# Dilated heads with the values as weights, and a mixture of dilations made on turned tiles

## The chip, the core and the metric

One Trainium2 chip, of which one core is used. The metric is the device time of one execution in microseconds. The engines are TensorE (PE, with PEld for the loading of its weights), VectorE (DVE), ScalarE (ACT), GpSimd (POOL) and SyncE (SP); POOL and SP issue DMAs here.

## What is computed

One layer of an encoder and its final norm, in float32, over 1280 tokens of 1024 features: a sample of 1024 tokens and a prompt of 256. The part that matters is the dilated branch and what follows it:

```
def _dilated_mixture(q, k, v, bias_b):
    outs, lses = [], []
    for gi, (window, dil) in enumerate(((128, 1), (512, 4), (2048, 16))):
        hs = slice(gi * 4, (gi + 1) * 4)
        o, lse = _banded_attention(residues(q[:, :, hs], dil), residues(k[:, :, hs], dil),
                                   residues(v[:, :, hs], dil), window // (2 * dil), dil, bias_b[:, hs], None)
        outs.append(from_residues(o, dil)); lses.append(from_residues(lse, dil))
    alpha = softmax(stack(lses), axis=0)
    return sum(alpha[..., None] * stack(outs), axis=0)

h = rmsnorm(x, g_mix); z = h @ w_in           # queries, keys, values of both branches, two gates
merged = gate_a * (o_a @ w_branch_a) + gate_b * (o_b @ w_branch_b)
x = x + merged @ w_out
x = x + square(relu(rmsnorm(x, g_mlp) @ w_up)) @ w_down
```

There are three groups (dilations 1, 4 and 16) of four heads of 64 features. `lse` is the maximum plus the logarithm of the sum of exponentials. The mixture weighs, for each token and each of the four heads, the three groups' outputs by the softmax of the three `lse`. The other branch, o_a, is an attention over a window of 128 with 8 heads.

## The kernel before

Large products are split into a high and a low part in the reduced format fp32r, three matmuls each (hi by lo, lo by hi, hi by hi), and those of w_in, w_up and w_down are combined in seven products for eight blocks. The work is written in the order in which it stands on each engine; generators that hand over with `yield` put one stage's steps between another's. The stages, by the profile's time: the norm and the values until about 120 us; pairs of columns of w_in until 355 us; the same pairs with the dilated heads between them until 535 us; the last pair until 560 us; windowed attention with the logits of the remaining gate columns as PE's filling until about 712 us; gates and branches until about 860 us; then w_out, w_up and w_down.

**The dilated heads** (`attention_b`, L482) have 60 tiles of 128 queries: an outer loop over the two pairs of heads i, then the groups 2, 1, 0, then the tiles of a group. Two tiles make a step, and a step is put at every second `tick` of the pairs' products. A step loads values for the present tiles (L503), multiplies the probabilities of the two tiles of two steps before with their values (`values_of`, L558), copies the results out and stores them (`store_values`, L570), turns the probabilities of the tiles before (L553, tile pt), and makes the scores (L522) and exponentials (L543) of the present ones. A tile's window is 128 or 256 keys wide; in group 2 a sample's tile consists of two pieces of 64 queries. In `values_of` the turned probabilities are PE's weights and the 64 columns of a head's values are streamed, so the result has queries in the partitions. Two tiles share a bank of PSUM (pv). A tile's results, its negated maxima (nm) and its sums (l) lie beside each other in a row of 132 numbers (o) and go to DRAM with one or two DMAs of POOL (L575) into `scr_b` of the group.

**Windowed attention** (from L1047) runs in a loop over j = 0, 2, ... 40 with two of 40 tiles each, four units of queries and ten tiles in a unit. In each iteration, in this order on PE: a part of the logits of the gates (`logits`, L1124, matmuls at L192), the values of an earlier tile (`values_of`, L1099; here the values are the weights, L1110, and the two heads of a pair have the upper and the lower half of the output's partitions), the turns (L1095), the scores (L1071), then the same for the second tile. Weights for the logits are split by ACT (whi, L231) and DVE (wlo, L235); ACT also makes the gates' column sums ready (gs, L1135), and the copies of turned probabilities are divided between ACT (L271) and DVE (L273).

**The mixture** runs beside that loop, a step at each half of an iteration from j = 4 on (`next(merges)`). For two tiles and one pair of heads, `load_rows` (L1140) fetches the rows of the three groups with eight DMAs of POOL for a sample's pair of tiles and six for the prompt's, each of them undoing the dilation; `merge` (L1162) makes the three weights of each row (L1167 to L1178, with the exponential on ACT), multiplies (L1182) and adds (L1187, L1188) on DVE. At the end of the loop and in the gate stage, PE turns the merged tiles (`turn_merged`, L1209, tile tm, 20 transposes), ACT makes the high part out of PSUM (L1224) and DVE the low part (L1228); both undo, in their order of columns, what the order of rows has left of the dilation. The gate stage puts these calls between its products by a table, `side`, from product number to calls.

POOL also issues the stores of windowed attention's results (`scr_o`, L1114) and the loads of its biases (L454 to L468), and makes the differences of w_in's blocks (L393). PSUM is handed out in banks by tag; "mm" is the tag of the large products.

Of the kernel before, what the change touches and what calls it, by code (L numbers as in the profile page):

```python
# [15 lines left out]
P = 128  # L16
# [3 lines left out]
T = NS + NP  # L20
# [9 lines left out]
ROW = 2 * HD + 4  # L30
# [67 lines left out]
def encoder_kernel(  # L98
# [97 lines left out]
    def run(gen):  # L196
        for _ in gen:
            pass
# [56 lines left out]
    l_a = const.tile([P, AH, NT], F32, name="l_a")  # L255

# [20 lines left out]
    scr_b = [dram.tile([T, 2, ROW], F32, name=f"scr_b{g}_") for g in range(3)]  # L277
# [204 lines left out]
    def attention_b(make):  # L482
# [5 lines left out]
        held, live, bias = {}, {}, {}  # L488
        turned_s = slot("pt", (P, 2, 4, P))
# [22 lines left out]
        def scores(j):  # L512
# [12 lines left out]
            for k in (j, j + 1):  # L525
# [5 lines left out]
                o = make("o", (P, ROW), n=8)  # L531
# [3 lines left out]
                nc.vector.tensor_scalar(o[:, 2 * HD : 2 * HD + 2], m, -1.0, None, op0=ALU.mult)  # L535
                live[k] = s, o

        def exponentials(j):
            W = order[j][3][1]
            s, o = live[j]  # L540
            nm, l = o[:, 2 * HD : 2 * HD + 2], o[:, 2 * HD + 2 :]
# [4 lines left out]
        def transposes(j, eng):  # L546
            W = order[j][3][1]
            s, o = live[j]
# [7 lines left out]
            live[j] = pt, o  # L556

        def values_of(j, whole):  # L558

            _, _, _, (pieces, W, _) = order[j]  # L560
            pt, v = live[j][0], held.pop(j)[1]
            pv = whole[:, P * (j % 2) : P * (j % 2) + P]
            for h in range(2):
                for a, (p0, nq, _, _) in enumerate(pieces):
                    for k in range(W // P):
                        nc.tensor.matmul(pv[p0 : p0 + nq, HD * h : HD * h + HD], pt[:, 2 * k + h, p0 : p0 + nq],  # L566
                                         v[:, a + k, HALVES[h]], start=k == 0, stop=k == W // P - 1,
                                         skip_group_check=True)

        def store_values(j, eng, whole):  # L570
            g, i, _, (pieces, _, _) = order[j]
            o = live.pop(j)[1]
            moved(eng, o[:, : 2 * HD], whole[:, P * (j % 2) : P * (j % 2) + P])
            for p0, nq, qa, _ in pieces:
                nc.gpsimd.dma_start(scr_b[g][qa : qa + nq, i, :], o[p0 : p0 + nq, :])  # L575
# [8 lines left out]
        for j in range(0, n + 4, 2):  # L584
            load_v(j)
            load_v(j + 1)
            if j > 2:
# [3 lines left out]
                store_values(j - 4, nc.scalar, pv)  # L591
                store_values(j - 3, nc.vector, pv)
# [456 lines left out]
    if True:  # L1049
# [90 lines left out]
        def load_rows(i, t):  # L1140

            r = rows_b[i, t] = wslot("r", (P, 2, 3, ROW))
            for j in range(2):
                if t < 8:
# [740 lines left out]
```

## Time and profile before

| | us |
|---|---|
| median of 3 runs | 1723.69 (1723.07 to 1723.81) |
| profiled execution | 1723.0 |
| its span, first to last instruction | 1721.2 |
| PE busy | 1690.8 |
| DVE, ACT, POOL busy | 973.6, 727.0, 516.2 |
| PE idle in the stage of windowed attention, 560 to 700 us | 2.23 of 140 |
| DVE, ACT, POOL busy in the same 140 us | 90.9, 81.7, 55.3 |

The granted clock of TensorE was 0.999 over the span. The profiled execution's time is 1.8 us more than its span, and 0.7 us below the median of the runs. In the profile, a line such as "L566 PE MATMUL pv<-v,pt x384" names a source line, an engine, an operation, the tile written and the tiles read; for PE the later tile of the two may be either the weights or what is streamed. [...] In the chain that ended last, each piece has a start, a length and a count; in the waits there stand a total, a count and the longest one.

### The profile page before, as it was taken

The numbers are of one execution on the slowest core, as the hardware profiler recorded it, in microseconds if no ns is written. First come the engines' busy times: TensorE is split into PE (matmuls) and PEld (weight loads), VectorE is DVE, ScalarE is ACT, GpSimd is POOL, SyncE is SP. The second block draws the span as 40 slices with busy tenths as digits, with TensorE's granted clock in tenths as the row PEclk, the third lists the DMA queues.
The fourth block names the chain that finished last, engine by engine and source line by source line (L and its number), as shares of the span: only waits on it lengthen the run. The fifth ranks groups of instructions, "written<-read, shape, count | busy, mean of one in ns | idle before, by whom it ended". The sixth has DMA issues, their size and how long they took to land.

```text
span 1721.2 us, 25157 instructions
## 1 busy us (share of the span) xinstructions
PE 1690.8 (98%) x9248; PEld 1430.4 (83%) x9248; DVE 973.6 (57%) x1688; ACT 727.0 (42%) x1528; POOL 516.2 (30%) x442
## 2 busy tenths in 40 slices
PE   7999999999999999999999999999999999999998
PEld 6898888888888888788888788888888888888886
DVE  6732323445553566677368545455556876667575
ACT  6232323355553555655166333333334433333344
POOL 0213222212322244300100445565555342314140
PEclk9999999999999999999999999999999999999999
DMA  6414343576666753656012334433446834633333
GB/s 239 145 43 140 115 137 95 150 196 178 173 171 176 208 174 104 221 181 230 25 74 74 122 120 157 149 115 127 157 136 232 308 130 158 209 115 117 117 116 123
DMA packets 213738, 256.34 MB, mean 149 GB/s; under 512 B 24487, under 2 KB 144123, under 8 KB 213488
## 3 DMA queue, kind: packets, MB, share of 16 engines
q1 hardware_dynamic: 200704, 228.26, 41.1%
q0 software_dynamic: 11824, 24.38, 4.6%
q10 hardware_dynamic: 1088, 2.10, 0.3%
q8 instruction: 73, 1.20, 0.3%
q14 instruction: 49, 0.40, 0.1%
HBM read 169.10 MB, written 90.73 MB: 151 GB/s over the span
## 4 chain that ended last, share of the span: by engine, by line
PE 87%; DVE 4%; ACT 2%; issue 2%; DMA 2%; POOL 1%; SPq 0%; DVEq 0%; ACTq 0%; POOLq 0%
PE dn L351 21%; PE x L351 18%; PE mm L192 12%; PE z L351 9%; PE v L739 5%; PE pv L351 5%; PE mm L351 5%; PE y L351 4%; PE pv L566 2%; PE sc L522 2%; PE pt L553 1%; PE pv L1110 1%; PE pt L1095 1%; PE tr L342 1%; DVE clo L318 1%
## 5 line engine op out<-in xcount | busy, mean ns | idle before, releaser
L351 PE MATMUL dn<-dhi,ulo 128*128 128x512 f32 x448 | 174.6, 390 | 2.9 <-DVE ulo L186 2.9
L351 PE MATMUL dn<-dlo,uhi 128*128 128x512 f32 x448 | 174.3, 389 | 0.0
L351 PE MATMUL dn<-dhi,uhi 128*128 128x512 f32 x448 | 174.3, 389 | 0.0
L351 PE MATMUL x<-chi,wlo 128*128 128x512 f32 x424 | 167.6, 395 | 2.0 <-DVE u L1760 1.4
L351 PE MATMUL x<-clo,whi 128*128 128x512 f32 x424 | 165.7, 391 | 0.1
L351 PE MATMUL x<-chi,whi 128*128 128x512 f32 x424 | 165.1, 389 | 0.0
L318 DVE TENSOR_TENSOR wlo<-ta,whi 128x1024 fp32r<-128x1024 f32 x30 | 55.7, 1857 | 180.9 <-ACT whi L316 180.9
L318 DVE TENSOR_TENSOR wlo<-raw,whi 128x1024 fp32r<-128x1024 f32 x60 | 89.4, 1491 | 102.2 <-ACT whi L316 102.2
L393 POOL TENSOR_TENSOR tb<-raw 128x512 f32<-128x512 f32 x25 | 33.6, 1345 | 340.8 <-PE mm L192 114.9
L351 PEld LDWEIGHTS dn<-dhi,ulo 128*128 128x128 f32 x448 | 84.1, 188 | 21.4 <-DVE ulo L186 3.9
L186 DVE TENSOR_TENSOR ulo<-uraw,uhi 128x1024 fp32r<-128x1024 f32 x56 | 95.2, 1720 | 11.7 <-ACT uhi L185 11.7
L351 PEld LDWEIGHTS dn<-dhi,uhi 128*128 128x128 f32 x448 | 84.1, 188 | 17.5
L351 PEld LDWEIGHTS dn<-dlo,uhi 128*128 128x128 f32 x448 | 84.1, 188 | 17.3
L351 PEld LDWEIGHTS x<-chi,wlo 128*128 128x128 f32 x424 | 79.7, 188 | 20.3 <-issue 3.1
L351 PEld LDWEIGHTS x<-chi,whi 128*128 128x128 f32 x424 | 79.6, 188 | 17.2
L351 PEld LDWEIGHTS x<-clo,whi 128*128 128x128 f32 x424 | 79.8, 188 | 14.8 <-DVE clo L318 0.4
L1585 POOL TENSOR_TENSOR t<-raw,t 128x1024 f32<-128x1024 f32 x16 | 46.0, 2897 | 143.1 <-DMA raw<-in_w_down_dram 143.1
L1736 DVE TENSOR_TENSOR v<-v,dn 128x512 f32<-128x512 f32 x90 | 59.5, 682 | 42.8 <-PE dn L351 38.7
L1832 POOL TENSOR_TENSOR u<-u,u 128x640 f32<-128x640 f32 x16 | 25.6, 1598 | 162.4 <-ACT u L1757 162.4
L351 PE MATMUL pv<-phi,wlo 128*128 128x256 f32 x256 | 72.5, 283 | 1.7 <-ACT u L1756 1.7
L351 PE MATMUL dn<-dhi,up 128*128 128x512 f32 x224 | 73.5, 389 | 0.0
L543 ACT ACTIVATE s<-s,o 128x128 f32<-128x128 f32 (+1 forms) x120 | 51.9, 434 | 50.5 <-DVE o L535 46.5
(338 smaller groups left out, 4724.2 us busy)
## 6 DMA issues: line engine op xcount, KB each, us to landing
scr_u<-u SPq DMA_DIRECT2D x112, 320.0 KB, 2.6
uraw<-scr_u SPq DMA_DIRECT2D x56, 512.0 KB, 4.2
raw<-in_w_in_dram SPq DMA_DIRECT2D x33, 512.0 KB, 6.0
raw<-in_w_up_dram SPq DMA_DIRECT2D x32, 512.0 KB, 5.4
raw<-in_w_down_dram SPq DMA_DIRECT2D x28, 512.0 KB, 6.5
sg<-scr_g SPq DMA_DIRECT2D x32, 256.0 KB, 6.2
uraw<-scr_u SPq DMA_DIRECT2D x28, 256.0 KB, 4.7
v<-scr_v SPq DMA_DIRECT2D x96, 64.0 KB, 2.4
```

Source lines behind the costliest of these rows:

```text
L186: nc.vector.tensor_tensor(lo, src, hi.bitcast(F32), op=ALU.subtract)
L192: nc.tensor.matmul(ps, a, b, start=i == 0, stop=i == len(seq) - 1)
L318: nc.vector.tensor_tensor(lo, src, hi.bitcast(F32), op=ALU.subtract)
L351: nc.tensor.matmul(ps, a, b, start=first and i == 0, stop=last and i == len(seq) - 1, skip_group_check=True)
L393: (nc.vector if vector else nc.gpsimd).tensor_tensor(o, x, y, op=ALU.subtract)
L522: nc.tensor.matmul(at(k, h)[p0 : p0 + nq, :], qk[rows, p0 : p0 + nq], qk[rows, P + P * a : P + P * a + W], start=True, stop=True, skip_gro ...
L543: nc.scalar.activation(s[:, h, :W], s[:, h, :W], AF.Exp, bias=nm[:, h : h + 1], accum_out=l[:, h : h + 1])
L566: nc.tensor.matmul(pv[p0 : p0 + nq, HD * h : HD * h + HD], pt[:, 2 * k + h, p0 : p0 + nq], v[:, a + k, HALVES[h]], start=k == 0, stop=k == ...
L739: nc.tensor.matmul(ps[:, :n], a, b, start=k == 0 and j == 0, stop=k == KC - 1 and j == 2)
L1585: nc.gpsimd.tensor_tensor(o, a, b, op=ALU.subtract)
L1736: nc.vector.tensor_tensor(v, v, ps, op=ALU.add)
L1832: nc.gpsimd.tensor_tensor(u[S1], u21, u22, op=ALU.add)
```

## The change

1. In `attention_b`, the values become PE's weights and the turned probabilities are streamed (L581). The result is turned: features of two heads in the partitions (64 each), queries in the columns. Two tiles share a bank as before; one copy of 128x256 takes both, alternately on DVE and ACT, into a tile of which there are three in place of eight (L598 stores it by runs of consecutive queries). `scr_b` has one array of 128 features by 1280 tokens for each group and pair of heads.
2. The negated maxima and the sums aren't stored with the rows. They stay in two tiles for the whole stage, `nm_b` and `l_b`, 128 partitions by 120 columns, a column for each tile and head (`places`).
3. All weights of the mixture are made at once at the beginning of windowed attention (`merge`). PE turns `nm_b` and `l_b` (L1180) into a bank of tag "mm", DVE copies both (L1182), POOL writes them to DRAM in the order of tokens with 13 DMAs (L1187, `scr_n`) and reads them back with 12 (L1204), so that the 40 columns of a partition hold all heads and each of the 128 partitions a share of the tokens. At j = 4 DVE puts groups 1 and 2 in the order of group 0 (L1209), makes the differences to the minimum (L1214 to L1216), and ACT the exponentials (L1217); half an iteration later DVE makes the weights (L1219 to L1232) and POOL stores them with six DMAs (`scr_c`, L1235).
4. The mixture itself has 18 items, by block of tokens (512, 512, 256), pair of heads and group. For each, POOL loads the values of the next item (L1250) and its weights, each head's row spread over 64 partitions (L1253 twice), multiplies the present item (L1267); DVE adds it to the block's sum in the following half of an iteration (L1271), reading it in the order that undoes the dilation.
5. The mixture being turned already, `turn_merged` goes; high and low parts are made by block with one instruction of ACT and one of DVE each (`high_b`, `low_b`), the first block's at j = n - 4 and the others' at 6, 7, 17 and 18 in the gate stage's table.
6. `sums_a` stands ahead of the rest of the mixture at the end of the loop.

The core of the diff (the generator `merge` is described above and cut to its first lines):

```
-        def values_of(j, whole):
+        def values_of(j, pv):
...
-            for h in range(2):
-                for a, (p0, nq, _, _) in enumerate(pieces):
-                    for k in range(W // P):
-                        nc.tensor.matmul(pv[p0 : p0 + nq, HD * h : HD * h + HD], pt[:, 2 * k + h, p0 : p0 + nq],
-                                         v[:, a + k, HALVES[h]], start=k == 0, stop=k == W // P - 1,
+            c = P * (j % 2)
+            for a, (p0, nq, _, _) in enumerate(pieces):
+                for k in range(W // P):
+                    for h in range(2):
+                        nc.tensor.matmul(pv[HALVES[h], c + p0 : c + p0 + nq], v[:, a + k, HALVES[h]],
+                                         pt[:, 2 * k + h, p0 : p0 + nq], start=k == 0, stop=k == W // P - 1,
                                          skip_group_check=True)
...
-        def load_rows(i, t):
...
-        def merge(i, t):
...
+        def merge():
+
+            cb = slot("cb")
+            ps = bank("mm", "tn")
+            for i, x in enumerate((nm_b, l_b)):
+                nc.tensor.transpose(ps[:ROWS, P * i : P * i + P], x, ident)
+            rows = cb[:ROWS, : 2 * P].rearrange("p (x q) -> p x q", x=2)
+            nc.vector.tensor_copy(rows, ps[:ROWS, : 2 * P].rearrange("p (x q) -> p x q", x=2))
...
+            def dump(r0, n, step, c0, m, base, stride):
+                dst = bass.AP(a.tensor, a.offset + base, [[stride, n], [ROWS * P, 2], [1, m]])
+                nc.gpsimd.dma_start(dst, rows[r0 : r0 + (n - 1) * step + 1 : step, :, c0 : c0 + m])
...
+            for g in range(3):
+                for b, sl in ((0, slice(0, 32)), (2, slice(32, 40))):
+                    R = place(g, b)[3]
+                    for x in range(2):
+                        dst = (raw[:, g, x, sl] if g else nat[:, x, 0, sl]).rearrange("p (r j) -> p r j", r=R)
+                        nc.gpsimd.dma_start(dst, spread(scr_n, g, b, x))
+            yield
...
+            for k, (b, i, g) in enumerate(items):
+                load(k + 1)
+                r = held.pop(k)
...
+                nc.gpsimd.tensor_tensor(r[:, 0, :] if g else m, r[:, 0, :], r[:, 1, :], op=ALU.mult)
+                yield
+                if g:
+                    m = m.rearrange("p (q r) -> p q r", r=R)
+                    nc.vector.tensor_tensor(m, m, r[:, 0, :].rearrange("p (r q) -> p q r", r=R), op=ALU.add)
+                yield
...
-        def turn_merged(t, tag="pt"):
...
+        def high_b(b):
...
+            nc.scalar.activation(ob_hi.t[b, 0], merged[b], AF.Copy)
...
-        merges = merges_of([(i, t) for t in range(0, NT, 2) for i in range(2)])
+        merges = merge()
         next(merges)
```

**PE, where windowed attention begins.** The rows of PE after the change, from the last product of the last pair (L355) over the two turns of nm_b and l_b to the first logits (L192) and scores (L1093):

```order
L355 MATMUL mm<-phi,whi 128x256
L1180 MATMUL tn<-ident,nm_b 120x128
L1180 MATMUL tn<-ident,l_b 120x128
L192 MATMUL mm<-hhi,wlo 128x512
L192 MATMUL mm<-hlo,whi 128x512
```

Before, L192's first row stood directly behind the last product; the two turns are new, and they take a bank of the tag that L192 uses.

**DVE, in the iteration j = 4.** The rows after the change, from the copy of windowed attention's values (L1135, L1113 before) to the next tiles' scores (L1095, L1073 before):

```order
L1135 COPY o<-pv 128x256
L1209 COPY cb<-cb 128x2x32
L1209 COPY cb<-cb 128x2x8
L1209 COPY cb<-cb 128x2x32
L1209 COPY cb<-cb 128x2x8
L1214 TENSOR_TENSOR cb<-cb 128x40
L1215 TENSOR_TENSOR cb<-cb 128x40
L1216 TENSOR_TENSOR cb<-cb 128x120
L235 TENSOR_TENSOR wlo<-raw,whi 128x1024
L275 COPY pt<-pt 128x256
```

In the place of L1209 to L1216 there stood the minima and the differences of the first two tiles (L1167 to L1170), which read rows loaded ahead of the loop.

**POOL, from the end of the pairs to the first products.** The rows after the change: the bias of the first unit, the 13 writes of nm_b and l_b, ten of the 12 reads, then in the second piece the last two of the six stores of weights, the loads of the first three items and two products:

```order
L458 DMA bias<-wide_1306 128x2x384
L1187 DMA scr_n<-cb 7x2x128 x4
L1187 DMA scr_n<-cb 4x2x64 x4
L1187 DMA scr_n<-cb 4x2x128
L1187 DMA scr_n<-cb 16x2x64 x2
L1187 DMA scr_n<-cb 16x2x128
L1187 DMA scr_n<-cb 48x2x128
L1204 DMA cb<-scr_n 128x32 x2
L1204 DMA cb<-scr_n 128x8 x2
L1204 DMA cb<-scr_n 128x4x8 x2
L1204 DMA cb<-scr_n 128x2x4 x2
L1204 DMA cb<-scr_n 128x8x4 x2
```

```order
L1235 DMA scr_c<-cb 128x8x4
L1235 DMA scr_c<-cb 128x2x4
L1136 DMA scr_o_92<-o 128x256
L1250 DMA r<-scr_b_83 128x512
L1253 DMA r<-scr_c 64x512 x2
L1250 DMA r<-scr_b_85 128x4x128
L1253 DMA r<-scr_c 64x4x128 x2
L1267 TENSOR_TENSOR merged<-r 128x512
L1136 DMA scr_o_93<-o 128x256
L1250 DMA r<-scr_b_87 128x8x64
L1253 DMA r<-scr_c 64x8x64 x2
L1267 TENSOR_TENSOR r<-r 128x512
```

A shape with three numbers is so many runs in each partition: 128x8x4 are 1024 runs of four numbers. Before, this queue held at the same place the eight loads of rows for the first call of `merge`, of 66 or 33 KB.

More of the change, by code (lines that the diff above doesn't have):

```diff
@@ L275, in encoder_kernel @@
     NH = AH + 3 * BH
-    scr_b = [dram.tile([T, 2, ROW], F32, name=f"scr_b{g}_") for g in range(3)]
+    scr_b = [[dram.tile([P, T], F32, name=f"scr_b{g}{i}") for i in range(2)] for g in range(3)]
+    scr_n = dram.tile([2, ROWS * P], F32, name="scr_n")
+    scr_c = dram.tile([1, ROWS * P], F32, name="scr_c")
     scr_o = [dram.tile([P, 4, 2, P], F32, name=f"scr_o{t}") for t in range(0, NT, 2)]
```

211 lines of the change are left out of this document (118 added, 93 removed).

## The prediction

> **What bounds the kernel now.** I read the busy times first, then the chain that ended last, then the table of windows from the dilated stage to the gates.
>
> ```profile
> span 1721.2 us, 25157 instructions
> PE 1690.8 (98%) x9248; PEld 1430.4 (83%) x9248; DVE 973.6 (57%) x1688; ACT 727.0 (42%) x1528; POOL 516.2 (30%) x442
> PE 87%; DVE 4%; ACT 2%; issue 2%; DMA 2%; POOL 1%; SPq 0%; DVEq 0%; ACTq 0%; POOLq 0%
> 450.00:500.00 50.00, 50.00 (x379) 41.48 (x377) 27.40 (x119) 29.11 (x102) 14.07 (x25) 1.00 0.68 190
> 500.00:535.00 35.00, 35.00 (x255) 29.75 (x254) 18.79 (x61) 16.99 (x52) 7.55 (x14) 1.00 0.47 140
> 560.00:600.00 40.00, 39.00 (x285) 33.04 (x284) 22.96 (x94) 21.59 (x61) 11.96 (x20) 1.00 0.70 208
> 600.00:650.00 50.00, 48.92 (x385) 41.38 (x384) 33.36 (x129) 30.05 (x83) 22.53 (x38) 1.00 0.58 167
> ```
>
> PE is busy for 98% of the span and carries 87% of the chain. A window's row gives its length, then the busy time of PE, weight load, DVE, ACT and POOL, the granted clock, and the share and rate of the DMA. The dilated stage (rows of 450 and 500) has no PE idle at all, with ACT at 29.11 of 50 us and DVE at 27.40: there a PE instruction removed is time removed. In windowed attention (from 560 on) PE stands still for 1 us of 40 and of 50. So **the order of the argument is**: PE work saved in the first stage, then whether the new mixture, which runs beside windowed attention, lets PE go on. Vector and POOL work count only if PE comes to wait for them.
>
> The profiled execution took 1723.0 us, 1.8 more than its span and 0.7 less than the median of the runs, 1723.7. The sum is made against 1723.0, and 0.7 is added at the end.
>
> **Dilated heads turned (L566 becomes L581): PE saves about 9 us.** Pieces of the chain, with start, length and count; the blocks of values in the dilated stage first (first and last of each size), then those of windowed attention, whose values already come turned (L1110):
>
> ```profile
> 365.29 0.84 PE pv L566 x8
> 499.95 0.84 PE pv L566 x8
> 390.83 1.22 PE pv L566 x16
> 530.13 1.22 PE pv L566 x16
> 420.10 1.73 PE pv L566 x16
> 518.97 1.73 PE pv L566 x16
> 421.83 0.88 PE pt L553 x8
> ...
> 581.28 0.93 PE mm L192 x4
> 582.21 1.46 PE pv L1110 x24
> 583.67 1.12 PE mm L192 x4
> 601.92 1.02 PE pv L1110 x16
> ```
>
> There are 30 steps: twelve of 0.84, twelve of 1.22 and six of 1.73 us, 35.1 in all. Eight instructions of L566 cost 0.84 or, from 16 against 8, 0.89: 0.11 each. For L1110, 24 against 16 gives 0.44 for eight, 0.055 each: two heads, in the two halves of the array's columns, run together. But a turned block has a fixed part: 1.02 less two times 0.44 is 0.14, and the L192 matmuls behind it take 1.12 where they take 0.93 elsewhere, 0.19 more; 0.33 in all. Of that, 0.12 is the longer modelled end of a 512-column matmul, which the present kernel pays too, later; 0.21 is left. The short instructions of the mixed blocks (1.22 less 0.84, 0.38 for eight) move 64 columns, and I take half of 0.44 for them. Then a block of 16 saves 1.73 - 0.88 - 0.21 = 0.64, a mixed one 1.22 - 0.44 - 0.22 - 0.21 = 0.35, one of eight 0.84 - 0.44 - 0.21 = 0.19: 3.8 + 4.2 + 2.3 = 10.3. With the whole 0.33 it is 6.7; with 0.14 as all that is paid it is 12.4. I take **9** between the lower two, since the blocks here are the short ones.
>
> [...]
>
> The two copies of a step become one and the stores get fewer; both are covered by the 20.9 us in 50 in which ACT idles. What is late next there is nothing but PE.
>
> **The turn of the merged tiles (L1216 to L1228) goes: 2.0 us.**
>
> ```profile
> L1216 PE MATMUL tm<-ident,merged x20: 270/272/332, 689.7 to 750.8; 128*128 128x128 f32 x20
> PE pt L1095 <- ACT pt L271: 1.2, 2, 0.7
> PE pt L1253 <- DVE o L1254: 0.9, 1, 0.9
> PE pt L1095 <- DVE pt L273: 0.7, 2, 0.5
> ```
>
> Twenty transposes go and two (tn, L1180) come; at the 0.11 of L553's row (0.88 for eight) that is 18 times 0.11. The lower three rows are PE's waits behind engines that also did the merging (total, times, longest): 2.8 us, some of which goes with 76 small loads on POOL and the merging on DVE. I take 0.8, bounds 0 and 2.8. **Gains together: 11.8 us.**
>
> **The weights of the mixture, all at once (L1180 to L1217): 9.8 us lost.** Here are the places where they are put, in the present kernel's clock, and what a POOL issue costs (mean ns):
>
> ```profile
> 560.48 0.40 PE L192 MATMUL mm<-hhi,wlo 128*128 128x512 f32 x1
> 562.84 0.60 ACT L936 ACTIVATE z<-x 128x512 f32<-128x512 f32 x1 [11.59 <-DMA hhi<-scr_h]
> 574.74 0.42 DVE L1113 COPY o<-pv 128x256 f32<-128x256 f32 x1 [1.21 <-PE pv L1110]
> 575.08 0.15 DVE L1167 TENSOR_TENSOR mm__5752<-r 128x4 f32<-128x4 f32 x1
> 575.66 0.21 ACT L1171 ACTIVATE e<-e 128x12 f32<-128x12 f32 x1 [0.71 <-DVE e L1170]
> 577.00 1.06 ACT L231 ACTIVATE whi<-raw 128x1024 fp32r<-128x1024 f32 x1 [0.85 <-DMA raw<-in_w_in_dram]
> 578.60 0.66 PE L1095 MATMUL pt<-ident,s 128*128 128x128 f32 x4 [0.51 <-ACT pt L271]
> ...
> L575 POOL DMA_DIRECT2D scr_b__82<-o x28 | 15.2, 546 | 43.0 <-ACT o L271 39.2 <-DVE o L273 3.8
> L454 POOL DMA_DIRECT2D bias<-wide x4 | 3.0, 752 | 14.2 <-issue 10.1 <-DMA r<-scr_b__82 2.5 <-DMA r<-scr_b__81 1.6
> ...
> scr_b__81<-o POOLq DMA_DIRECT2D x16, 66.0 KB, 2.0
> scr_o<-o POOLq DMA_DIRECT2D x5, 128.0 KB, 5.0
> r<-scr_b__82 POOLq DMA_DIRECT2D x12, 33.0 KB, 6.3
> ```
>
> The chain is: two transposes at 560.5, one copy to 561.7, 13 dumps on POOL, 12 spread loads on POOL that wait for them, then DVE's four copies (L1209) and ACT's exponential (L1217). A dump is priced like a store of up to 128 runs, 0.53 to 0.55 us: 13 take 7, to 568.7, and the last has landed 2.2 later, at 570.9 (the landing of quiet stores; the DMA rows give 2.0 quiet and 5.0 in this stretch). A load of 256 runs (bias) issues in 0.75 where 128 runs take 0.55: 0.2 per 128 runs, so 1.1 for 512 and 2.0 for 1024. Of the 12 loads four have 128 runs, four 256, two 512 and two 1024: 2.2 + 3.0 + 2.2 + 4.0 = 11.4, to 582.3, and 2.7 to land (towards the quiet end, since the burst is dying down): **585.0**. No row has such short runs (32 to 128 bytes): at 0.55 a load and landings of 1.8 it would be 578, at the 5 and 6.3 of the DMA rows and one slot waited for, 592.
>
> [...]
>
> Who waits: DVE reaches L1209 at 575.2, right behind the copy of the values. Queued behind it are L235 and the scores of the next tiles; behind ACT's exponential stand gs, whi (577.00) and the copy pt, for which PE's transposes wait at 578.6. PE has only what is queued ahead of them. From the last landing on the same 3.2 us follow as now from 575.2 to PE's start. So 585.0 - 575.2 = 9.8 us of standstill, bounds 2.8 and 16.8. The bank of tn is the one that the first L192 takes at 560.48 now, so that matmul will wait for ACT to empty another one (z, 562.84): 2.4 us. They delay what comes ahead of the hole and not its end, which POOL's chain sets, and so they are inside the 9.8; in the hidden case they are most of what is lost.
>
> **The first products of the mixture: 4.2 us lost.** One step of the loop lasts 6.7 us (values at 582.21, and by the next row here 588.92); the first DVE add (L1271) stands in the step after the next, behind the copy at 596.70.
>
> ```profile
> 588.92 1.46 PE pv L1110 x24
> 596.70 0.42 DVE L1113 COPY o<-pv 128x256 f32<-128x256 f32 x1 [1.35 <-PE pv L1110]
> L393 POOL TENSOR_TENSOR tb<-raw 128x512 f32<-128x512 f32 x25 | 33.6, 1345 | 340.8 <-PE mm L192 114.9
> ```
>
> Between the weights and that add POOL issues, in order, six stores of weights (0.55 twice, 0.75 twice, 1.1, 2.0: 5.7), a scr_o (0.6), the loads of the first three items (1.7, 2.6, 4.2: each one of the values and two of weights over 64 partitions, by runs as above), another scr_o and two products at 1.35 (L393): 18.1 us, against 14.2 from the weights to the add. With a landing in the chain I put the loss at 4.2; if the short runs issue at 0.55 it is 0.5, and with the 5 to 6.3 us landings 8. Afterwards POOL has 1.7, 2.6 or 4.2 for loads, 1.35 for the product and 0.6 for scr_o in 6.7 us: at most 6.1. It keeps up, barely, and the loads of the next two units fall on it: 1.5 us, bounds 0 and 3. The twelve adds on DVE, and six wide ACT and DVE instructions for the split, replace more work than they are (33.36 of 50 busy in the row of 600), at nothing. SP's queue has nothing new. sums_a moves ahead of the mixture's remainder, one add, whose reader (high_b of the last block) stands 17 jobs of the gate stage later: nothing waits.
>
> **Sum.** -9 - 2.0 - 0.8 + 9.8 + 4.2 + 1.5 = +3.7: 1726.7 against 1723.0, and 1727.4 as a median.
>
> **Rivals.** *The chain is hidden.* Short runs cost no more than the rows of 0.55, the landings stay at 1.8 to 2.0: the weights come 2.8 late and the first add 0.5: -11.8 + 3.3 = -8.5, 1715.2. For it: the quiet landings. Against it: the stretch from 560 to 580 carries a burst of weights, keys and queries, and 25 issues at 0.55 alone take 13.8 us where there are 13.5 from 561.7 to 575.2.
> *POOL decides (the other side).* From 6.7 us of POOL work per step on, the products set the pace of the loop. With the landings of the DMA rows the weights are 16.8 late, the first add 8 and the later bursts 3: -11.8 + 27.8 = +16.0, 1739.7. For it: 4.2 us of an item with 1024 runs is an extrapolation from 256, and it stands 0.6 under the point.
> *The short blocks gain nothing.* If entering and leaving each cost the 0.33, the 30 steps take 0.66 each beside their stream (six of 0.88, twelve of 0.66, twelve of 0.44: 18.5), 38.3 against 35.1: 3.2 lost instead of 9 won, 1739.6. [...]
>
> **How the numbers follow.** Forecast 0.45 (its own range 1721 to 1734); hidden 0.30; POOL decides 0.17; no gain from short blocks 0.08. The likeliest gives 1727.4. The range 1713 to 1741 takes in the hidden case and both slow ones at their centres. A measurement of this kernel can tell about 0.2%, 3.4 us, from no change. Faster by more: the hidden case nearly whole and a little of the forecast, 0.32. Within: 0.24, from the forecast. Slower by more: the rest of it and the two slow cases, 0.44.
>
> **What would show it.** L581 in the chain at 26 us where L566 has 35; PE without idle until the stage begins; one hole in PE between 575 and 590 that ends with DVE's L1209 behind a load of cb from scr_n; a second, of 4 us, that ends with DVE's L1271 behind POOL's product. No first hole: hidden. Holes in every step: POOL decides. I am wrong at the root if the hole lies before 570 or the blocks of L581 don't get shorter.

## The result and the profile after

The changed kernel takes 1726.01 us (median of 14 runs, 1722.74 to 1728.47), the kernel before 1723.12 (14 runs, 1721.64 to 1725.10): a ratio of 1.0016, with a 95% interval of 1.0008 to 1.0024, so 2.9 us more, against 3.7 forecast. The profiled execution took 1727.48 us with a span of 1725.3. The sum was right; two of its terms weren't, and two losses that it doesn't hold stand against a gain that it held too small.

First the busy times, then windows: three that were shown of before, and the stretch of PE's hole; columns as there (length, PE, weight load, DVE, ACT, POOL, granted clock, DMA).

```profile
PE 1682.3 (98%) x9230; PEld 1413.3 (82%) x9230; DVE 965.1 (56%) x1565; ACT 718.8 (42%) x1485; POOL 527.6 (31%) x451
450.00:500.00 50.00, 50.00 (x385) 37.73 (x385) 29.19 (x126) 28.57 (x98) 11.31 (x20) 1.00 0.67 195
560.00:600.00 40.00, 28.88 (x218) 24.28 (x218) 16.83 (x66) 16.91 (x47) 22.80 (x35) 0.83 0.51 132
572.55:586.20 13.65, 5.10 (x16) 3.68 (x18) 6.79 (x28) 3.91 (x9) 6.44 (x10) 0.50 0.28 53
600.00:650.00 50.00, 48.28 (x387) 40.63 (x382) 31.31 (x90) 28.31 (x78) 30.40 (x40) 1.00 0.76 235
```

PE is 8.5 us less busy than before (1690.8), and the time is longer all the same. The window from 560 to 600 has 28.88 us of PE where it had 39.00, and a clock of 0.83: there is one hole, and PE comes out of it at half its clock.

To see where time goes, take one PE instruction in both traces (the same tile and shapes, in the same order) and subtract its start before from its start now. This shift, at seven places of the trace of before, for the changed kernel and for all that follows (us; the last column is the difference of the two before it; except in e12, nearly all of it arises at the beginning of the w_down products):

| | 341: ahead of the dilated stage | 540: behind it | 600: behind the hole | 650 | 760: behind the turns | 1322: ahead of w_down | 1700 | w_down |
|---|---|---|---|---|---|---|---|---|
| changed | +0.85 | -8.32 | +3.95 | +4.61 | -0.26 | -0.39 | +4.42 | 4.8 |
| changed again (e1) | +0.49 | -8.69 | +3.22 | +2.91 | -1.23 | -1.37 | +2.42 | 3.8 |
| mixture late (e2) | +0.34 | -8.84 | -10.44 | -2.79 | -5.25 | -5.30 | -3.05 | 2.3 |
| hole filled (e3) | +0.96 | -7.91 | +4.06 | +4.72 | -0.08 | -0.23 | +2.99 | 3.2 |
| heads apart (e4) | +0.38 | -0.42 | +12.33 | +10.84 | +6.62 | +6.53 | +11.48 | 5.0 |
| chain early (e5) | +0.11 | -8.86 | -9.11 | -8.66 | -13.04 | -12.90 | -8.77 | 4.1 |
| mixture later (e7) | +0.94 | -8.24 | -9.84 | -10.38 | -4.81 | -4.88 | -0.46 | 4.4 |
| early, with a gap (e8) | +0.98 | -7.98 | -8.30 | -10.74 | -15.59 | -15.44 | -10.83 | 4.6 |
| e8, one scratch (e11) | +0.36 | -8.62 | -8.94 | -11.37 | -16.05 | -15.90 | -11.79 | 4.1 |
| e11, loads swapped (e12) | +0.67 | -8.30 | -8.60 | -11.03 | -15.33 | -15.14 | -13.83 | 1.3 |
| before again (e6) | +0.58 | +0.58 | -0.36 | -1.23 | -0.85 | -0.99 | -0.96 | 0.0 |
| before, spare array (e9) | +0.62 | +0.62 | -0.29 | -1.13 | -0.81 | -0.93 | -0.94 | 0.0 |

The row of e6 says how far two executions of the same program differ: up to 1.8 us, nearly all within windowed attention. That of e9 is nearly the same program.

**The dilated stage: 9.2 us gained** (from +0.85 to -8.32). The blocks of values in the chain that ended last, the first of each size:

```profile
366.17 0.59 PE pv L581 x8
391.20 0.82 PE pv L581 x16
418.81 1.02 PE pv L581 x16
```

They stand there twelve, twelve and six times: 23.0 us where there were 35.1. (The counts are of instructions: L581 has 384 in the trace for 192 products of the source.) Of these 12.1 us the stage keeps 9.2; 0.1 us per step is lost behind a block.

**The hole: 12.1 us lost between 578 and 583 of the trace of before.** The chain that ended last, from the turn of nm_b to PE's way out, and what POOL's queue did:

```profile
552.33 0.23 PE tn L1180 x2
...
554.49 6.83 DMA scr_n<-cb
...
562.11 5.21 DMA scr_n<-cb
...
567.39 3.24 issue
570.63 3.00 POOL cb L1204 x5
...
576.02 2.07 DMA cb<-scr_n
```

```profile
L1204 POOL DMA_DIRECT2D cb<-scr_n x12 | 8.3, 696 | 5.3 <-issue 4.2 <-DMA scr_n<-cb 1.0
570.63 6.11 POOL L1204 DMA_DIRECT2D cb<-scr_n  x8 [4.25 <-issue]
scr_n<-cb POOLq DMA_DIRECT2D x4, 7.0 KB, 6.4
581.10 1.79 PE L1117 MATMUL pt<-ident,s 128*128 128x128 f32 x6 [11.12 <-ACT pt L273]
```

The writes to DRAM landed after 5.2 to 6.8 us, beside a burst of loads (e5 below has the same writes outside it); the reads came when that was over, and the last of them landed in 2.07. In the last row of the second piece is the wait: 11.12 us on PE, until ACT's copy pt (L273), which stands behind the exponential of the weights. Its end, 581.10, is 2.50 later than the same instruction before (578.60), so the wait costs 10.6; the next values start 3.93 later, 1.4 more, at a clock of 0.50. These 1.4 us are the clock's: PE runs without a pause there (busy for 5.10 us of the 5.10 from 581.10 to 586.20), and the same matmuls begin 0.42 us apart, where before (first two rows) it was 0.23.

```profile
581.12 0.40 PE L192 MATMUL mm<-hhi,whi 128*128 128x512 f32 x1
581.35 0.40 PE L192 MATMUL mm<-hhi,wlo 128*128 128x512 f32 x1
584.13 0.63 PE L192 MATMUL mm<-hhi,whi 128*128 128x512 f32 x1
584.55 0.63 PE L192 MATMUL mm<-hhi,wlo 128*128 128x512 f32 x1
```

**The first products: 3.1 us, beside a gain of 2.4.** Between 600 and 650 the shift grows by 0.7 us only. But e8 below, in which DVE waits for no product, gains 2.4 us in the same stretch, and against e8 the changed kernel loses 3.1 there (from 12.25 to 15.35; in e1 it is 2.1). DVE waits at its first two adds, and PE's scores wait behind the second:

```profile
602.67 1.10 DVE L1271 TENSOR_TENSOR merged<-merged,r 128x512 f32<-128x512 f32 x1 [1.63 <-POOL r L1267]
610.95 1.04 DVE L1271 TENSOR_TENSOR merged<-merged,r 128x512 f32<-128x512 f32 x1 [3.13 <-POOL r L1267]
PE sc L1093 <- DVE m L1095: 1.3, 1, 1.3
```

**The start of the w_down products: 4.8 us lost, 577 us behind the last instruction of a changed line (L1289, at 750.2).** DVE and POOL there, first before, then after, and PE's waits:

```profile
1327.35 4.54 DVE L186 TENSOR_TENSOR ulo<-uraw,uhi 128x1024 fp32r<-128x1024 f32 x2
1327.94 6.20 POOL L1585 TENSOR_TENSOR t<-raw 128x1024 f32<-128x1024 f32 x2 [4.65 <-DMA raw<-in_w_down_dram]
PE dn L351 <- DVE ulo L186: 2.1, 2, 1.7
```

```profile
1326.88 5.11 POOL L1643 TENSOR_TENSOR t<-raw 128x1024 f32<-128x1024 f32 x2 [3.38 <-DMA raw<-in_w_down_dram]
1326.95 2.85 DVE L1819 SCALAR_TENSOR_TENSOR u<-u 128x512 f32<-128x512 f32 x1
1329.72 5.84 DVE L186 TENSOR_TENSOR ulo<-uraw,uhi 128x1024 fp32r<-128x1024 f32 x2
PE dn L355 <- DVE ulo L186: 5.4, 1, 5.4
1332.00:1336.00 4.00, 2.87 (x7) 2.20 (x8) 4.00 (x3) 1.46 (x2) 3.92 (x2) 0.50 0.17 67
```

Before, POOL's subtraction begins 0.59 us behind DVE's first ulo. After, it begins 0.07 ahead of DVE's L1819, which takes 2.85 us in place of 0.69; the ulo come 2.4 later, PE waits 5.4 us in place of 2.1, and the clock falls to 0.50 once more.

### The profile page after: what moved, and what is told of

It is laid out like the page before. It is cut to its first block, busy times and chain, and to the rows that moved or that the text cites. A ratio compares the mean times of both kernels' runs of the same rounds, so it can differ in the third digit from the quotient of the medians.

```text
span 1725.3 us, 24932 instructions
## 1 busy us (share of the span) xinstructions
PE 1682.3 (98%) x9230; PEld 1413.3 (82%) x9230; DVE 965.1 (56%) x1565; ACT 718.8 (42%) x1485; POOL 527.6 (31%) x451
## 4 chain that ended last, share of the span: by engine, by line
PE 85%; issue 8%; DMA 2%; DVE 2%; POOL 1%; ACT 1%; SPq 0%; POOLq 0%; DVEq 0%; ACTq 0%
PE dn L355 21%; PE x L355 18%; PE mm L192 10%; PE z L355 9%; PE v L761 6%; PE mm L355 5%; PE pv L355 5%; PE y L355 4%; PE sc L538 2%; PE pv L581 1%; PE pt L568 1%; PE pv L1132 1%; DMA r<-scr_c 1%; PE pt L1117 1%; DMA scr_n<-cb 1%
## 5 line engine op out<-in xcount | busy, mean ns | idle before, releaser
L355 PE MATMUL dn<-dhi,ulo 128*128 128x512 f32 x448 | 175.3, 391 | 6.1 <-DVE ulo L186 6.1
L355 PE MATMUL dn<-dlo,uhi 128*128 128x512 f32 x448 | 175.0, 391 | 0.0
L355 PE MATMUL dn<-dhi,uhi 128*128 128x512 f32 x448 | 175.0, 391 | 0.0
L355 PE MATMUL x<-chi,wlo 128*128 128x512 f32 x424 | 167.6, 395 | 2.1 <-DVE u L1818 1.4
L355 PE MATMUL x<-clo,whi 128*128 128x512 f32 x424 | 165.8, 391 | 0.1
L355 PE MATMUL x<-chi,whi 128*128 128x512 f32 x424 | 165.1, 389 | 0.0
L355 PEld LDWEIGHTS dn<-dhi,ulo 128*128 128x128 f32 x448 | 84.6, 189 | 24.6 <-DVE ulo L186 7.0
L355 PEld LDWEIGHTS dn<-dlo,uhi 128*128 128x128 f32 x448 | 84.5, 189 | 17.6
L355 PEld LDWEIGHTS dn<-dhi,uhi 128*128 128x128 f32 x448 | 84.5, 189 | 17.5
L355 PEld LDWEIGHTS x<-chi,wlo 128*128 128x128 f32 x424 | 79.7, 188 | 20.5 <-issue 3.1
L355 PEld LDWEIGHTS x<-chi,whi 128*128 128x128 f32 x424 | 79.6, 188 | 17.2
L355 PEld LDWEIGHTS x<-clo,whi 128*128 128x128 f32 x424 | 79.8, 188 | 14.8 <-DVE clo L322 0.4
L558 ACT ACTIVATE s<-s,nm_b 128x128 f32<-128x128 f32 (+1 forms) x120 | 51.9, 434 | 54.5 <-DVE nm_b L550 54.5
L355 PE MATMUL pv<-phi,wlo 128*128 128x256 f32 x256 | 72.5, 283 | 1.7 <-ACT u L1814 1.7
L355 PE MATMUL dn<-dhi,up 128*128 128x512 f32 x224 | 73.5, 389 | 0.0
```

The lines of the kernel that those rows point to most:

```text
L355: nc.tensor.matmul(ps, a, b, start=first and i == 0, stop=last and i == len(seq) - 1, skip_group_check=True)
L558: nc.scalar.activation(s[:, h, :W], s[:, h, :W], AF.Exp, bias=nm[:, h : h + 1], accum_out=l[:, h : h + 1])
```

## The experiments

**e1: the changed kernel again, unaltered.**

> The changed kernel unaltered, for a second profiled execution. Two things are to be told apart: what belongs to the change, and what belongs to one execution. If the hole of PE in windowed attention belongs to the change, it stands again at 567 to 581 us, 10 to 12 us long, with the granted clock at 0.5 behind it. For the second hole, at the start of the w_down products (5.4 us behind DVE's ulo, clock 0.5), theory A: it is an accident of that execution, where DVE's and POOL's instructions met; then it is nearer to the 1.7 us of the kernel before here, and the span is up to 4.5 us shorter (1721 to 1723). Theory B: it follows from the change; then it stands here again, 5 us, span 1725.

1725.43 us (11 runs), ratio 1.0015 (1.0006 to 1.0024). The first hole stands again, 10.8 us, at the same transposes. At w_down the growth is 3.8 us: less than 4.8, but not near the 0.0 between the two executions of the kernel before. So theory B is the nearer one; no row of the table settles yet how the change reaches so far.

**e2: the mixture two iterations later.**

```
                 values_of(*order[j - 4])
-                if j < n:
+                if 6 < j < n:
                     next(merges, None)
...
                 transposes(*order[j - 1])
-                if j > 2:
+                if j > 6:
                     next(merges, None)
```

> The steps of the mixture begin at j = 8 in place of j = 4, two iterations (13.4 us) later; nothing is left out. My theory: the hole is only the wait of DVE (L1209) and ACT (L1217) for the loads of cb, which land at 578.1 while DVE is there at 567; two iterations later DVE is there at about 580, so hole and clock drop go, and PE is 11 to 12 us earlier behind them: the median 10 us under the changed kernel, 1714 to 1717, if the items left over at the end of the loop are hidden by the gate stage. Rival: the time is lost anyway, because POOL gets its 25 DMAs and the products into one stretch with the load bursts: a hole of 5 us or more appears further on, or at the end of the loop, and the median stays within 4 us of the changed kernel.

1721.34 us, ratio 0.9989 (0.9980 to 0.9997). The hole goes: at 600 the shift is -10.44. Seven us of it come back 20 us later. In this kernel DVE's first add, PE's wait, the clock behind it, and the landings of the first products' loads:

```profile
DVE merged L1271 <- POOL r L1267: 7.8, 1, 7.8
PE pt L1117 <- DVE pt L275: 6.9, 1, 6.9
606.00:612.00 6.00, 1.94 (x7) 1.76 (x8) 4.37 (x10) 0.82 (x3) 4.86 (x7) 0.50 0.73 207
r<-scr_b POOLq DMA_DIRECT2D x2, 256.0 KB, 10.9
r<-scr_c POOLq DMA_DIRECT2D x4, 128.0 KB, 10.1
```

Theory and rival both hold in part. The hole is the wait for the chain; but the first loads now fall on the loads of the next unit, land after 10 us, and the term that I had put at 4.2 costs 7 here.

**e3: the hole filled with PE work.**

```
+            if j == 4:
+                ps, w = bank("pv", "fill"), h_at(0, 0, 512)[0]
+                for _ in range(40):
+                    nc.tensor.matmul(ps, w[:, :P], w, start=True, stop=True)
             if j:
                 transposes(*order[j - 1])
```

> Forty matmuls whose result nobody reads (128x512 in fp32r, 0.23 us each, 9.3 us in all) stand on PE at the place of the hole, ahead of the transposes that wait. Theory: after the hole the clock stands at 0.5 for some 5 us because PE was idle, and this costs 1.4 us (the shift against the kernel before is 10.6 us at the first transpose behind the hole and 12.0 at the next values). With the filling the clock stays at 1.0 and PE is 1.4 us earlier at those values, median 1 to 2 us under the changed kernel. Rival: behind the hole DVE and ACT set the pace and not the clock; then the shift stays at 12.0 and the median doesn't move.

1725.01 us, ratio 1.0007 (0.9998 to 1.0016); it can't be told from e1. PE's wait shrinks to 1.9 us, but the values behind it are no earlier (+4.06, where the changed kernel has +3.95), and the clock still falls to 0.50 for a shorter time, behind a stretch in which PE was busy for 1.09 of 3.41 us:

```profile
579.27:582.68 3.41, 1.09 (x7) 0.62 (x6) 1.83 (x3) 2.58 (x5) 0.00 (x0) 1.00 0.41 146
582.68:586.09 3.41, 3.41 (x10) 2.44 (x8) 3.24 (x18) 1.33 (x5) 0.57 (x2) 0.50 0.02 5
```

The forecast fails, since the clock fell with the filling too, which ended 1.9 us ahead of the transposes. As a test of the theory the median says nothing, but the rows do: all of PE's work from the scores to the values (582.93 to 586.19) falls into the 3.41 us at 0.50, in which PE is busy throughout, and takes 3.26 us where it took 1.96 before. The rival, that DVE and ACT set the pace there, doesn't fit a PE without a pause.

**e4: the two heads apart.** All first heads of a step, then all second heads:

```
-            for a, (p0, nq, _, _) in enumerate(pieces):
-                for k in range(W // P):
-                    for h in range(2):
+            for h in range(2):
+                for c, pieces, W, pt, v in both:
+                    for a, (p0, nq, _, _) in enumerate(pieces):
+                        for k in range(W // P):
```

> In the dilated stage the first heads of both tiles come before the second heads of both, where the change has the two heads in turn; instructions, operands and shapes are the same. Theory: the 9.2 us that the stage gains come from two heads that run together in the two halves of the array's columns; with the heads apart only the pair in the middle of a block overlaps, so the gain shrinks to 0 to 2 us, and windowed attention begins 7 to 9 us later than with the change (at 560 in place of 552 us). Rival: the gain is that of the narrower weights (64 columns to load where there were 128); then it keeps most of the 9.2 and windowed attention begins within 3 us of the changed kernel.

1733.38 us, ratio 1.0061 (1.0047 to 1.0074). The stage gains 0.8 us (from +0.38 to -0.42) in place of 9.2, so the gain is two heads that run together, and not the narrower weights. The blocks in this kernel:

```profile
420.19 1.51 PE pv L580 x16
439.64 1.31 PE pv L580 x14
450.90 0.59 PE pv L580 x8
```

The long ones go from 1.02 to 1.51 and the mixed ones from 0.82 to 1.31. The short ones stay at 0.59, which I hadn't expected and can't explain from the rows.

**e5: the chain of the weights early.** `place`, `spread` and `merge` stand ahead of `tick`, and the first step of `merge` is taken when the dilated stage has ended:

```
             if n > 0 and n % 2:
-                next(att_b, None)
+                if next(att_b, 1) and att_b.gi_frame is None and not early:
+                    early.append(merge())
+                    next(early[0])
...
-            ps = bank("mm", "tn")
+            ps = bank("pv", "tn")
...
-        merges = merge()
-        next(merges)
+        merges = early[0]
```

> The turn of nm_b and l_b, the 13 writes and the 12 reads stand right behind the last step of the dilated stage, some 19 us of PE's work ahead of windowed attention (the bank is one of tag pv in place of mm); all else stays, the products too. My theory: the hole is the wait for this chain and nothing else, so it goes with its clock drop; PE is 11 to 12 us earlier behind it than in the changed kernel, and what is left is about 1 to 3 us of waiting for the first products while the next unit's loads run. Median 1713 to 1717. Rival (the one that the later start of the mixture has just shown): the wait only moves to the first products, whose loads are stretched by the next unit's loads: then the gain behind the first products is under 6 us, median 1719 to 1722.

1715.23 us, ratio 0.9955 (0.9943 to 0.9968). Neither hole nor drop of the clock: at 600 the shift is -9.11, 12 to 13 us better than in the changed kernel. That the hole is this chain is shown. The turns begin 27 us earlier here (525.1 in place of 552.2), which hides it; e2 hides it by using the weights 13.4 us later, and how little would do wasn't tried. The same writes land in 1.6 to 1.7 us here, ahead of the burst, but for the last and largest of them (48 KB, 4.6). The products still wait, on DVE twice, and PE 2.1 us:

```profile
scr_n<-cb POOLq DMA_DIRECT2D x4, 7.0 KB, 1.7
DVE merged L1150 <- POOL r L1146: 5.5, 2, 3.4
PE sc L1210 <- DVE m L1212: 2.1, 2, 1.8
```

**e7: the mixture four iterations later than in the change**, at j = 12 (the edit of e2 with 10 for 6).

> The steps of the mixture begin at j = 12, an iteration after the next unit's loads are issued (j = 10). With the start at j = 8 the first product waited 7.7 us on DVE, since its loads took 10 to 11 us beside those of the next unit. Theory: the collision is one of place; at j = 12 the weights' stores and the first loads land in 2 to 4 us, and no hole of over 3 us is left in windowed attention; four items are left for the end of the loop, which the gates hide. Median 1713 to 1717. Rival: POOL's chain of 18 us from the weights to the first add is too long for the 14.2 us of the loop wherever it stands; then a hole of 4 us or more stands at the first add here too, median 1718 to 1722.

1721.39 us, ratio 0.9991 (0.9982 to 1.0000). In the loop the theory holds: no hole, -10.38 at 650. The hiding at the end doesn't: the copies wl of `widen` stand on POOL behind the items left over, and PE waits for them. So the median misses the 1713 to 1717 that the theory had.

```profile
PE pt L1314 <- POOL wl L1304: 6.1, 1, 6.1
```

**e8: the early chain, and a gap between weights and products.** Weights at j = 2, products as before:

```
             if j > 2:
                 values_of(*order[j - 4])
-                if j < n:
-                    next(merges, None)
+            if 0 < j < n:
+                next(merges, None)
...
                 transposes(*order[j - 1])
-                if j > 2:
-                    next(merges, None)
+                next(merges, None)
...
+            yield
+            yield
             yield
             items = [(b, i, g) for b in range(3) for i in range(2) for g in range(3)]
```

> As the early chain, and the weights are made at j = 2 in place of j = 4, with two empty steps ahead of the first products, which stay where they are (j = 6). It gives the stores of the weights a further 6.7 us to land before the first loads. Theory: if POOL's chain from weights to the first add (18 us against 14.2) is what is left after the early chain, this takes it away, and the median is 1 to 3 us under that of the early chain: 1711 to 1715. Rival: the loads of the products are held up by the next unit's loads and not by the stores of the weights; then it is the same as the early chain within 1 us.

1712.24 us, ratio 0.9935 (0.9922 to 0.9947), 3 us under e5. In windowed attention DVE has no wait for a product left in its list, and PE's three waits add up to 1.1 us, of which the longest is

```profile
PE pt L1236 <- DVE pt L275: 0.5, 1, 0.5
```

So the way from the weights to the first add was the second cost. It is worth 3 us with the early chain, and by the shifts 2.1 to 3.1 in the changed kernel too.

**e6: the kernel before, again, unaltered.**

> The kernel before, unaltered, for a second profiled execution of it. At the start of the w_down products it lost 2.1 us behind DVE's ulo in the first one, where five executions of changed kernels have lost 2.6 to 5.4 us. If that place varies by execution, it shows something between 2 and 5 us here; if the shift of time that the change brings makes it worse, it shows 2 us again. Median 1723.

1722.98 us, and at w_down 2.2 us of waits and no growth. Two executions of before agree there; all of the changed kernels so far, whatever their shift, grow by 2.3 to 5.0. It is the change, then. What of it?

**e9 and e11: addresses in DRAM.** The change moves the scratch arrays behind scr_b by 61,440 bytes. e9 moves them in the kernel before, e11 moves them back in e8 (`scr_c = scr_n`):

```
     scr_b = [dram.tile([T, 2, ROW], F32, name=f"scr_b{g}_") for g in range(3)]
+    spare = dram.tile([1, 120 * P], F32, name="spare")
...
         sums_a()
+        nc.gpsimd.dma_start(spare[:, :P], ident[:1, :])
```

> The kernel before with a spare array of 61,440 bytes in DRAM behind scr_b (written once with 512 bytes, off the path), so that every scratch array behind it, scr_u among them, has the address that it has in the changed kernel. Both executions of the kernel before lose 2.1 to 2.2 us at the start of the w_down products, all eight of changed kernels 2.6 to 5.4, and the landings of the scr_u stores are the first times that differ there. Theory: the change moves scr_u by 61,440 bytes and with it the times at which the transfers land; then this kernel loses 3 us or more at that place and its span is 2 to 5 us over the 1720 to 1721 of before, median 1725 to 1727. Rival: something else of the change does it (addresses in SBUF, the lengths of the engines' programs); then 2 us there and a median of 1723.

> The early chain with the gap, and the weights are stored into the array that nm_b and l_b were written to (scr_n, long since read) and not into one of their own, so that scr_u and all else behind it has the address of the kernel before. If the address theory holds, the loss at the start of the w_down products (4.6 us of shift in the run without this) goes back to near nothing, and the median is 1708 to 1709 where that run has 1712.2. Rival: the address has no part in it, and the median stays within 1 us of 1712.

e9: 1722.42 us, ratio 0.9998 (0.9989 to 1.0006), no growth at w_down. e11: 1711.25 us, ratio 0.9931 (0.9917 to 0.9944), a growth of 4.1. The theory of addresses falls, twice.

**e12: the loads at w_down in another order.**

```
         def begin(self):
...
+            self.fetch(*JOBS[1])
             self.block(1, 0, 0)
             self.block(1, 0, 1)
...
-            self.fetch(*JOBS[1])
             yield
```

> The early chain with the gap and one scratch array, and at the start of the w_down products SP issues the next uraw loads ahead of the four raw loads that POOL's third subtraction (t) waits for, not behind them. In the three executions of the kernel before, that subtraction begins 0.6 us after DVE's first ulo, and two ulo take 4.54 us; in all executions of changed kernels but one it begins 0.15 to 0.5 us ahead of it, and two ulo take 6.7. Theory: whichever of the two begins first holds up the other, and the 2.2 us on DVE, with the clock drop behind them, are the 2 to 5 us that every changed kernel loses there. With the raw loads some 1.5 us later POOL is behind again: two ulo at 4.5 us or less, and the median 2 to 4 us under the 1711.25 of that kernel. Rival: the subtraction being later only moves the collision to the next DVE instructions, and the median stays within 1 us of 1711.

1709.27 us (1709.04 to 1709.38), ratio 0.9917 (0.9903 to 0.9930): the best of all, 14 us under the kernel before, and 2.0 under e11, at the lower edge of what was expected. DVE and POOL there, in e11 and in e12:

```profile
1311.28 5.78 POOL L1648 TENSOR_TENSOR t<-raw 128x1024 f32<-128x1024 f32 x2 [3.91 <-DMA raw<-in_w_down_dram]
1311.43 6.71 DVE L186 TENSOR_TENSOR ulo<-uraw,uhi 128x1024 fp32r<-128x1024 f32 x2
1317.00:1321.00 4.00, 3.01 (x8) 2.22 (x8) 4.00 (x3) 2.11 (x2) 3.92 (x3) 0.50 0.15 59
```

```profile
1312.21 2.35 DVE L186 TENSOR_TENSOR ulo<-uraw,uhi 128x1024 fp32r<-128x1024 f32 x2
1315.47 4.76 POOL L1648 TENSOR_TENSOR t<-raw 128x1024 f32<-128x1024 f32 x2 [7.33 <-DMA raw<-in_w_down_dram]
1317.00:1321.00 4.00, 4.00 (x19) 3.32 (x18) 2.00 (x1) 1.80 (x2) 4.00 (x3) 1.00 0.00 0
```

In e12 the subtraction begins when both ulo are done: they take 2.35 us, not 6.71, and the clock stays at 1.00. The rows fit two engines that take turns, a whole instruction each. Alone, one ulo takes 1.18 us (half of 2.35) and one subtraction 2.40 (the first in e11, at 1301.62, which begins while DVE is idle). In the kernel before, the first ulo takes 1.22 us and the second, begun 0.55 behind POOL's start, 3.40; ulo, subtraction, ulo and subtraction end at 1328.57, 1330.81, 1331.89 and 1334.14, so 2.24, 1.08 and 2.25 us apart. With POOL first, as in e11, two of each in turn make 7.2, and from 1311.28 to the end of the second ulo it is 6.86; with DVE first, as before, ulo, subtraction and ulo make 4.8, and it is 4.54. So the loss at w_down is that the two engines meet there, and it is larger when POOL comes first. Why they take turns, no run shows.

Right behind this place e12 is 6 us better off than e11; 3 of them go again within 30 us. There the two engines don't meet, since POOL is idle (third row); DVE waits for a load of v, and PE for the ulo behind it:

```profile
1341.11 0.69 DVE L1799 TENSOR_TENSOR v<-v,dn 128x512 f32<-128x512 f32 x1 [2.37 <-DMA v<-scr_x]
PE dn L355 <- DVE ulo L186: 2.4, 3, 1.6
1335.00:1340.00 5.00, 5.00 (x24) 4.14 (x23) 2.08 (x3) 4.53 (x5) 0.00 (x0) 1.00 1.06 385
```

With its subtraction later, POOL's next work ends at 1330.26 where it ended at 1326.52, and SP's stores and loads follow later. This is the price of the other order of loads. Why POOL's third subtraction begins 0.7 to 1.3 us earlier, against DVE, in the kernels with the change, its loads landing earlier, stays open; the addresses in DRAM are not the reason, and other placings weren't tried.

## Why the prediction was right in its sum

The measured change, 2.9 us, is also less than the 3.4 us that the prediction takes as the least that can be told from no change, an outcome to which it gave 0.24. The first two terms were right with their mechanism. That the rest adds up is luck.

- *The dilated stage*, 9 forecast, 9.2 measured, with the mechanism that was argued (e4). The prices held one by one: a block of 16 was to take 0.88 + 0.14, and takes 1.02; one of eight 0.58, and takes 0.59; a mixed one 0.80, and takes 0.82.
- *The weights of the mixture*, 9.8 forecast, 10.6 measured for the wait and 12.1 with what follows it. The place, the engines and the order were right. The arrival of the weights was put at 585.0 in the clock of before, and came at 578.1 in a kernel 8.3 us ahead, 586.4. Inside, errors cancel. The writes were taken to land in 2.2 us and took 5.2 to 6.8 in the burst; behind them POOL stood 3.24 us for which the profile names nothing. The reads were taken to issue in 11.4 us, all behind the last write, and took 8.3: by my 0.2 us per 128 runs the eight longer ones should have taken 9.2 and took 6.11, and the four shorter ones were issued while the last writes were still landing.
- *What follows the wait*, 1.4 us, had no term. It is the clock at 0.50, as the rows of PE show.
- *The first products and the later bursts*, 5.7 forecast, are a step that was mis-sized: 3.1 measured (2.1 in e1), against e8. POOL's way from the weights to the first add was 17.3 us (585.33 to 602.67) where I had 18.1; but the loop came late as well, at half clock, so that DVE stood only 1.63 us at the first add. At the second it stood 3.13, behind loads that took some 6 us. e2 and e8 show that the term is real: 7 us when the loads fall on the next unit's, 3 us when the hole is gone.
- *The turns and PE's small waits*, 2.8 forecast, are the other. From 650 to 760 the shift falls by 4.9 us (4.1 in e1), and with the 2.4 that the products hide, e8 has 7.3 from 600 to 760. The 18 transposes are 2.0 of them. What I allowed for the engines that were relieved, 0.8, was too small, and so was its upper bound, 2.8, the sum of the waits that the profile lists. The list leaves out short ones, since a matmul's modelled end covers them (L192 at 581.12 in the trace of before is 0.40 us long, and the next one begins 0.23 behind its start): behind 648 it has 0.22 us, while the shift of e8 falls by 0.6. Which engine's relief gives how much isn't shown.
- *The w_down products*, 3.8 to 4.8 us, weren't in the sum at all. Nothing of the change touches that stage, and I had looked at no window beyond 860 us. The forecast holds because some 2.6 us too much at the products and 4.5 too little at the turns and waits make up for this and for the clock, 6.2 us together.
- The rivals: the chain wasn't hidden (in e5 it is; that its 1715.23 meets that rival's 1715.2 is chance, since the other terms differ), POOL didn't set the pace (30.40 us of 50), and the short blocks gained what they should. My sign of a root error, a hole ahead of 570, was badly put: it begins at 570, because the stage begins 8 us earlier.

## What to carry to other kernels

Data that pass through DRAM should start as soon as they exist, and not where they are used: the same 28 instructions cost 12 us at the head of a stage full of loads and nothing 27 us earlier. A sum of gains on a PE-bound kernel needs the holes after it: with those of 11.1 and 5.4 us in the changed kernel and of 6.9 in e2 the clock fell to 0.50 each time, and stayed there for some us behind them (until 586.20 with PE at work from 581.10 on), and where two engines meet by a few tenths of a us, a change can turn their order around hundreds of us later, even in a kernel that is by then no more than 0.4 us ahead. A small wait that the profile lists can stand for a larger one. Compare the shift of the same instruction along the whole trace before believing that the sum of a change is the change.

## What the runs showed of the hardware

One window of the changed kernel, in the burst of loads at the beginning of windowed attention, and one of e5, where the same writes are issued ahead of it:

```profile
560.00:564.00 4.00, 4.00 (x33) 4.00 (x32) 1.49 (x6) 2.77 (x8) 2.91 (x6) 1.00 1.11 371
526.00:533.00 7.00, 7.00 (x39) 6.04 (x39) 4.18 (x5) 3.82 (x5) 6.73 (x13) 1.00 0.10 27
```

Stores of 2 to 48 KB from POOL took 5 to 7 us to land while 371 GB/s were under way, and those up to 16 KB 1.6 to 1.7 us at 27 GB/s. That they were small didn't help: in the burst it was 5.9 us for 2 KB and 5.3 for 48 KB.

PE stops at 570 in the changed kernel, its clock is at 0.50 from 572.55 to 586.20, though work resumes at 581, and full behind that. The stretches at 0.50 last 13.65 us here, 6.83 at w_down (1330.31 to 1337.14), about 10.3 in e2 (clocks of 0.94, 0.50 and 0.70 in the three windows of 6 us from 600 to 618) and 3.41 in e3: near four, two, three and one times 3.41. In e3 a wait of only 1.9 us on PE was followed by such a stretch; in e5 one of 1.8 was not (clock 1.00 from 590 to 600), nor the one of 1.7 at w_down in the kernel before (1.00 from 1328 to 1336).
